# A scan kernel on one core: state work placed between the large operations, and Ln, Exp and output in three successive slots

## The chip, the core and the metric

The kernel runs on one core of a Trainium2 chip. The metric is the device time of one execution in microseconds (us). Each time below is the median of three to seven executions of the same kernel; runs that are compared were made in turn on the same chip. An execution can fall into a slower state (over 1.5% above the fastest of its kernel). Medians are over all runs, ratios over the fast ones alone.

A profile names the engines PE (matmul), PEld (PE's weight loads), DVE (the vector engine), ACT (the scalar engine), POOL and SP. "L303" is line 303 of the kernel that the profile belongs to, so the numbers differ between kernels; the tile names do not.

## The reference

A recurrence over 2048 steps for 16 batch rows of 256 channels. Everything is float32.

```python
for b in range(batch):                        # 16
    aa, bb, pp = zeros, zeros, -1e38          # vectors of 256
    for t in range(seq_len):                  # 2048
        ww = u + k[b, t];  qq = maximum(pp, ww)
        e1, e2 = exp(pp - qq), exp(ww - qq)
        output[b, t] = (e1 * aa + e2 * v[b, t]) / (e1 * bb + e2 + 1e-08)
        ww = pp - w + k[b, t];  qq = maximum(ww, k[b, t])
        e1, e2 = exp(ww - qq), exp(k[b, t] - qq)
        aa, bb, pp = e1 * aa + e2 * v[b, t], e1 * bb + e2, qq
```

## The kernel before

The steps are cut into 16 states of 126 steps (two halves of 63) and a head of 32 steps. A state has four *pairs*; a pair is two tiles of two batch rows, so 126 x 1024 numbers of k and as many of v. The kernel goes through 66 pairs in *slots*, one new pair a slot. Four slots are one state, and the time from one state to the next is called the *period*.

In slot n the new pair goes through PE (X: two matrices times k give the logs of the weights), ACT (exp of X into the tile `ez`), DVE (`ez` times v) and PE again (`tot`: sums over the steps, collected over the four pairs of a state). Ten slots later (`LAG`) the same pair is output: `den` and `num` are matmuls over `ez`, ACT takes Ln of `den` and Exp of minus that (`rd`, the reciprocal), DVE multiplies by `num`, and POOL stores.

```python
    LAG = 10
    ...
    kpool = ctx.enter_context(tc.tile_pool(name="kpool", bufs=AHEAD))
    ezpool = ctx.enter_context(tc.tile_pool(name="ezpool", bufs=7))
    rpool = ctx.enter_context(tc.tile_pool(name="rpool", bufs=5))
    ...
            for t, x, eng in ((kr, k, SP if n <= AHEAD else POOL), (vr, v, SP)):   # loads of a pair
                K(eng.dma_start(
                    out=t[0:r, :, :], in_=x[4 * p:4 * p + 4, t0:t0 + r, :].rearrange("n t d -> t n d")))
```

Between the two, the sums of a state become the state that enters it. That is *state work*, a chain of some twenty small operations: `copy_sums` (ts, ACT), `turn_sums` (a transposition on PE into a `den` tile), `split_sums` (tsum, DVE), `state_logs` (lf, ACT), offsets and `near` (DVE), `state_weights` (w and g, ACT), `tb`, `da`, `AB` (DVE), `inject_logs` and `inject_weights` (y and phi, ACT), `carries` (DVE), `turn_carries` (PE). The state is written as two rows below the 126 steps of `ez`, by four small transfers of 8 KB each, on the queue that also brings v:

```python
    def inject(c):
        row = small.tile([128, 128], BF16, tag="row", name="row")
        K(DVE.tensor_copy(row, st.pop((c, "d"))[:, 0:128]))
        for j in range(2):
            for h in range(2):
                p = 64 * h + 32 * j
                K(SP.dma_start(out=EZ[group_of(c, j)][TC + h:TC + h + 1, 0:2, :, :].rearrange(
                                   "o q i (x c) -> o (q i x) c", c=128),
                               in_=row[p:p + 32, :]))

    def den(n):                                    # reads all 128 rows of ez: the carried rows too
        rl, ri = (NH, NH) if is_head(n) else (128, TC)
        d = bank("den", [128, 2, D])
        ...
    def recip(n):                                  # Ln, then Exp of it, at once
        ...
            K(SC.activation(rd[0:r, a, :], d[0:r, a, :], ACT.Ln, scale=RS))
            K(SC.activation(rd[0:r, a, :], rd[0:r, a, :], ACT.Exp, scale=-1.0))
```

In the timelines each engine works in exactly the order in which the program is written. With s the last slot of a state (its first pair was slot s-3, so it is output from slot s-3+10 = **s+7** on), the order of a steady slot and the places of the state work are:

```python
        work += [(s + 1, "last", split_sums), (s + 2, "first" if c else "exp", state_logs),
                 (s + 2, "sums", state_offsets), (s + 2, "sums", state_weights), (s + 2, "pool", first),
                 (s + 2, "act", inject_logs), (s + 3, "exp", inject_weights),
                 (s + 3, "pool", carries), (s + 3, "last", turn_carries), (s + 3, "last", inject)]
    ...
    for n in range(NP + LAG + 1):
        ...
        exps(n);  small_work(n, "exp");  sums(n - 1);  round_k(n + 1);  small_work(n, "sums")
        num(qp, 0);  den(q);  recip(q);  mult(qp, 0);  num(qp, 1);  small_work(n, "pool")
        times_v(n);  mult(qp, 1);  store(qp);  logs(n + 1);  cast_v(n + 1)
        small_work(n, "dve");  small_work(n, "act");  small_work(n, "last")
```

(That loop is shortened: conditions for the first and last slots are left out.)

Of the kernel before, what the change touches and what calls it, by code (L numbers as in the profile page):

```python
# [7 lines left out]
F32 = mybir.dt.float32  # L8
# [14 lines left out]
def kernel(  # L23
# [363 lines left out]
    def state_offsets(c):  # L387
        lf = st.pop((c, "lf"))
        for h in range(2):
            i = 2 * c + h  # L390
            K(DVE.scalar_tensor_tensor(S[:, i + 1], S[:, i], 0.0, lf[:, h], ALU.max, ALU.add))
        near = tiny.tile([128, 3, 32], F32, tag="near", name="near")
        K(DVE.tensor_scalar(near, S[:, 2 * c:2 * c + 3], NEAR, -NEAR, ALU.min, ALU.max))
        st[c, "near"] = near
# [24 lines left out]
    def state_step(c, h):  # L419
        if h == 0:  # L420
            t = st.pop((c, "t"))[:, 0:4].rearrange("p (q h) x -> p q h x", q=2)
            tb = small.tile([128, 2, 2, 32], F32, tag="tb", name="tb")
            K(DVE.scalar_tensor_tensor(tb, by_two(st.pop((c, "w"))), 1.0, t, ALU.min, ALU.mult))  # L423
            st[c, "tb"] = tb
        cur = AB[c]
        if h == 1:
            AB[c + 1] = small.tile([128, 2, 2, 32], F32, tag="AB", name="AB")
        da = tiny.tile([128, 2, 32], F32, tag=f"da{h}", name=f"da{h}")
        K(DVE.tensor_add(da, cur[:, :, h], st[c, "tb"][:, :, h]))
        K(DVE.scalar_tensor_tensor(cur[:, :, 1] if h == 0 else AB[c + 1][:, :, 0], by_two(st[c, "g"][:, h + 1]), 1.0,  # L430
                                   da, ALU.min, ALU.mult))
# [11 lines left out]

    def carries(c):

        ab = tiny.tile([128, 4, 2, 16], BF16, tag="ab16", name="ab16")
        f, f2 = st.pop((c, "phi")), tiny.tile([128, 2, 32], F32, tag="phi2", name="phi2")
        K(DVE.scalar_tensor_tensor(f2, st[c, "g"][:, 0:2], 1.0, f, ALU.max, ALU.min))
# [43 lines left out]
    def recip(n):  # L492
        r = NH if is_head(n) else TC
        i = tiles_of(n)
        rd = rpool.tile([128, 2, D], F32, tag="rd", name="rd")
        d = DEN.pop(n)
        for a in ((0, 1), (1, 2)) if n == NP - 1 else ((0, i),):
            a = slice(*a)
            K(SC.activation(rd[0:r, a, :], d[0:r, a, :], ACT.Ln, scale=RS))  # L499
            K(SC.activation(rd[0:r, a, :], rd[0:r, a, :], ACT.Exp, scale=-1.0))  # L500
        RD[n] = rd
# [36 lines left out]

    later = {}
    for c in range(-1, NST):  # L540
        s = last_of[c]
        work = [(s + 1, "sums", copy_sums), (s + 1, "last", turn_sums)]
        first, second = lambda c: state_step(c, 0), lambda c: state_step(c, 1)
        if c < 0:
            work += [(s + 2, "sums", split_sums), (s + 2, "act", state_logs),
                     (s + 3, "exp", state_weights), (s + 3, "pool", state_start)]
        else:
            work += [(s + 1, "last", split_sums), (s + 2, "first" if c else "exp", state_logs),
                     (s + 2, "sums", state_offsets), (s + 2, "sums", state_weights), (s + 2, "pool", first),
                     (s + 2, "act", inject_logs), (s + 3, "exp", inject_weights),  # L550
                     (s + 3, "pool", carries), (s + 3, "last", turn_carries), (s + 3, "last", inject)]
            if c + 1 < NST:
                work.append((s + 4 if c else s + 3, "pool", second))
            else:

                work = [(s + 1, "act", copy_sums), (s + 2, "sums", turn_sums), (s + 2, "sums", split_sums),
                        (s + 3, "first", state_logs), (s + 3, "sums", state_offsets), (s + 3, "act", state_weights),
                        (s + 3, "last", first), (s + 4, "act", inject_logs), (s + 4, "act", inject_weights),
                        (s + 4, "last", carries), (s + 5, "pool", turn_carries), (s + 5, "pool", inject)]
        for slot, where, f in work:  # L560
            later.setdefault((slot, where), []).append((f, c))

    def small_work(n, where):
        for f, c in later.pop((n, where), []):
            f(c)

    for slot, where, f in ((0, "exp", matrices_for_sums), (1, "pool", matrices_for_head),
                           (4, "dve", matrices_for_outputs),
                           (5, "dve", more_matrices_for_outputs)):
        later.setdefault((slot, where), []).append((lambda c, f=f: f(), None))  # L570
# [9 lines left out]
    for n in range(NP + LAG + 1):  # L580
        q, qp = out_at.get(n), out_at.get(n - 1)
        live, out_q, out_qp = n < NP, q is not None, qp is not None
# [4 lines left out]
        small_work(n, "first")  # L587
        if live:
            exps(n)
        elif out_q:  # L590
            den(q)
            recip(q)
        small_work(n, "exp")
        if 0 < n <= NP:
            sums(n - 1)
# [57 lines left out]
```

## Time and profile before

| | before |
|---|---|
| median of 3 runs (range) | 331.96 us (329.77 to 335.51) |
| span of the profiled run, mean granted clock | 332.9 us, 0.983 |
| period (copies of the sums, start to start) | 17.76 to 17.77 us, once 17.99 |
| rows issued, and needed | end of slot s+3, slot s+7: about 13 us later |

The prediction below shows the views that carry its argument. First the busy share per engine and, from the same page, the chain that ended last (what released what, followed back from the end; shares of the span by engine, then by line):

```profile
PE 284.7 (86%) x1183; PEld 136.8 (41%) x1200; DVE 284.4 (85%) x571; ACT 277.8 (83%) x310; POOL 114.0 (34%) x162
...
PE 43%; DVE 27%; DMA 10%; ACT 10%; issue 6%; SPq 1%; POOL 0%; POOLq 0%; DVEq 0%; ACTq 0%
PE X L287 12%; PE num L509 11%; PE tot L349 10%; DMA vr<-in_v_dram 7%; DVE ez L319 6%; PE den L488 5%; DVE rd L517 5%; DVE km L271 5%; ACT ez L303 5%; PE den L365 4%; DVE vb L311 4%; DMA kr<-in_k_dram 3%; DVE tsum L372 2%; ACT rd L499 1%; DVE tb L423 1%
```

Three engines are within 3% of each other, and the chain wanders over all of them; the only transfers of any size in it are v loads, nearly all of it the last ones (7%), and the first k loads (3%). Of the rows only one of the last is in it, with 2.8 us. Second, the transfers by kind (destination from source, queue, how many, KB each, median us from issue to landing), and under it the view of the row tile in the steady part, 85 to 265 us (minimum, median, maximum to landing):

```profile
vr<-in_v_dram SPq DMA_DIRECT2D x60, 512.0 KB, 5.1
...
ez<-row SPq DMA_DIRECT2D x64, 8.0 KB, 6.4
```

```profile
DMA to landing us min/median/max: 5.0/6.5/7.2
```

In the steady part 8 KB take 6.5 us, where the first rows of the run, at 44 us, land after 1.9; with about 13 us of distance, 7.2 us is hidden. The 5.1 of the v loads must not be set beside it: the trace tells the landing of six v loads only, all issued in the first 26 us.

### The profile page before, as it was taken

What the parts mean: (1) busy time and instruction counts of PE and PEld (TensorE: products, weight loads), DVE (VectorE), ACT (ScalarE), POOL (GpSimd) and SP (SyncE); (2) the same over time, 40 slices, a digit from 0 to 9 for tenths busy, and PEclk for the clock granted to TensorE, in tenths of its full rate; (3) what the DMA queues carried; (4) which work ended last, traced back from release to release, by engine and by line L of the source; (5) the groups of instructions that cost most, each with busy time, mean ns of one, the idle gap of its engine ahead of it and who ended that gap; (6) DMA issues with size and microseconds to landing.
All of it is one profiled execution on the core that took longest, in us unless ns stands there. A gap on an engine that the chain in (4) does not pass through costs nothing.

```text
span 332.9 us, 4061 instructions
## 1 busy us (share of the span) xinstructions
PE 284.7 (86%) x1183; PEld 136.8 (41%) x1200; DVE 284.4 (85%) x571; ACT 277.8 (83%) x310; POOL 114.0 (34%) x162
## 2 busy tenths in 40 slices
PE   0786988799999998999999999999998999599580
PEld 0333544344445453545454444444453445234230
DVE  2888798989898989999999989898989997777560
ACT  2656699699999999998999999999999997798780
POOL 6211224514243434425243434243334433022231
PEclk9999799999999999999999999999999999999987
DMA  7999859899999999999999999999999999545855
GB/s 251 227 348 349 280 184 323 254 326 321 341 366 343 375 336 372 328 364 347 376 343 374 344 365 348 349 368 343 364 342 373 317 274 322 196 130 166 252 166 166
DMA packets 59120, 102.47 MB, mean 308 GB/s; under 512 B 7610, under 2 KB 43162, under 8 KB 59098
## 3 DMA queue, kind: packets, MB, share of 16 engines
q0 software_dynamic: 19232, 65.27, 56.2%
q1 hardware_dynamic: 39858, 36.93, 36.5%
q8 instruction: 9, 0.15, 0.2%
q14 instruction: 13, 0.11, 0.1%
q10 hardware_dynamic: 8, 0.00, 0.0%
HBM read 68.10 MB, written 33.55 MB: 305 GB/s over the span
## 4 chain that ended last, share of the span: by engine, by line
PE 43%; DVE 27%; DMA 10%; ACT 10%; issue 6%; SPq 1%; POOL 0%; POOLq 0%; DVEq 0%; ACTq 0%
PE X L287 12%; PE num L509 11%; PE tot L349 10%; DMA vr<-in_v_dram 7%; DVE ez L319 6%; PE den L488 5%; DVE rd L517 5%; DVE km L271 5%; ACT ez L303 5%; PE den L365 4%; DVE vb L311 4%; DMA kr<-in_k_dram 3%; DVE tsum L372 2%; ACT rd L499 1%; DVE tb L423 1%
## 5 line engine op out<-in xcount | busy, mean ns | idle before, releaser
L535 POOL DMA_DIRECT2D out_dram<-rd x64 | 58.6, 916 | 173.6 <-ACT rd L500 79.3
L303 ACT ACTIVATE ez<-X 128x2048 bf16<-128x2048 f32 x58 | 107.9, 1860 | 4.4 <-PE X L287 4.4
L517 DVE TENSOR_TENSOR rd<-num,rd 126x512 f32<-126x512 f32 (+1 forms) x131 | 89.1, 686 | 9.1 <-issue 3.4
L319 DVE TENSOR_TENSOR ez<-ez,vb 126x2048 bf16<-126x2048 bf16 (+1 forms) x66 | 79.9, 1211 | 2.4 <-ACT ez L301 1.8
L499 ACT ACTIVATE rd<-den 126x1024 f32<-126x1024 f32 (+2 forms) x67 | 67.0, 1000 | 9.0 <-PE den L488 8.3
L500 ACT ACTIVATE rd<-rd 126x1024 f32<-126x1024 f32 (+2 forms) x67 | 69.6, 1039 | 2.1
L287 PE MATMUL X<-km,NLE 128*128 128x512 f32 x128 | 52.6, 493 | 14.9 <-DVE km L271 13.8
L128 POOL DMA_DIRECT2D kr<-in_k_dram x61 | 47.8, 784 | 30.3 <-DVE km L271 11.6
L349 PE MATMUL tot<-ez,OHV 126*48 126x512 bf16 x128 | 50.1, 391 | 8.3 <-DVE ez L319 8.3
L509 PE MATMUL num<-ez,LfN 128*128 128x512 bf16 x128 | 49.5, 387 | 6.5 <-DVE rd L517 6.3
L349 PE MATMUL tot<-ez,OHE 128*48 128x512 bf16 x128 | 51.1, 399 | 0.0
L509 PE MATMUL num<-ez,IdN 126*128 126x512 bf16 (+1 forms) x131 | 50.3, 384 | 0.0
L271 DVE CAST km<-kr 126x1024 fp32r<-126x1024 f32 x64 | 44.8, 700 | 4.5 <-ACT km L205 4.5
L311 DVE CAST vb<-vr 126x1024 bf16<-126x1024 f32 (+1 forms) x66 | 45.4, 688 | 3.6 <-DMA vr<-in_v_dram 3.6
L287 PE MATMUL X<-km,NLZ 128*128 128x512 f32 x128 | 41.0, 403 | 0.0
L488 PE MATMUL den<-ez,Id 126*128 126x512 bf16 (+1 forms) x131 | 39.6, 382 | 0.9
L488 PE MATMUL den<-ez,Lf 128*128 128x512 bf16 x111 | 34.9, 383 | 5.3 <-DMA ez<-row 2.3
L287 PEld LDWEIGHTS X<-km,NLE 128*128 128x128 f32 x128 | 24.1, 196 | 27.4 <-DVE km L271 9.5
L287 PEld LDWEIGHTS X<-km,NLZ 128*128 128x128 f32 x128 | 24.7, 193 | 6.1 <-ACT ez L301 0.3
L349 PEld LDWEIGHTS <-OHE 128*48 128x48 bf16 x128 | 13.2, 104 | 33.6 <-issue 26.9
L509 PEld LDWEIGHTS <-LfN 128*128 128x128 bf16 x128 | 12.4, 97 | 32.1 <-issue 23.2
L509 PEld LDWEIGHTS <-IdN 126*128 126x128 bf16 (+1 forms) x131 | 12.9, 98 | 23.7 <-issue 21.9
(101 smaller groups left out, 205.0 us busy)
## 6 DMA issues: line engine op xcount, KB each, us to landing
out_dram<-rd POOLq DMA_DIRECT2D x63, 504.0 KB, 7.2
vr<-in_v_dram SPq DMA_DIRECT2D x60, 512.0 KB, 5.1
kr<-in_k_dram POOLq DMA_DIRECT2D x57, 512.0 KB, 7.9
vr<-in_v_dram SPq DMA_DIRECT2D x4, 504.0 KB
kr<-in_k_dram POOLq DMA_DIRECT2D x4, 504.0 KB, 11.3
kr<-in_k_dram SPq DMA_DIRECT2D x3, 512.0 KB, 6.5
ez<-row SPq DMA_DIRECT2D x64, 8.0 KB, 6.4
kr<-in_k_dram SPq DMA_DIRECT2D x3, 128.0 KB
```

Source lines behind the costliest of these rows:

```text
L271: K(DVE.tensor_copy(KM[n][0:r, 0:i, :], kr_of.pop(n)[0:r, 0:i, :]))
L287: K(PE.matmul(X[q][:, i, :], m[0:kr, :], km[0:kr, i, :], start=True, stop=True))
L303: K(SC.activation(ez_of(n)[:, 0:4:2], X[2][:, :, 0:i, :], ACT.Exp))
L311: K(DVE.tensor_copy(vb[0:r, 0:i, :], vr_of.pop(n)[0:r, 0:i, :]))
L319: K(DVE.tensor_mul(ez[0:r, 1:4:2], ez[0:r, 0:4:2], vb[0:r, 0:i, :].unsqueeze(1).broadcast_to([r, 2, i, D])))
L349: K(PE.matmul(TOT[c], m[0:r, :], ez_of(n)[0:r, q, i, :], start=n == first_of[c] and i == 0 and q == 0, stop=n == last_of[c] and i == tiles ...
L488: K(PE.matmul(d[:, i, :], m[0:r, :], ez_of(n)[0:r, q, i, :], start=q == 0, stop=q == 2, skip_group_check=True))
L499: K(SC.activation(rd[0:r, a, :], d[0:r, a, :], ACT.Ln, scale=RS))
L500: K(SC.activation(rd[0:r, a, :], rd[0:r, a, :], ACT.Exp, scale=-1.0))
L509: K(PE.matmul(d, m[0:r, :], ez_of(n)[0:r, q, i, :], start=q == 1, stop=q == 3, skip_group_check=True))
L517: K(DVE.tensor_mul(RD[n][0:r, i, :], NUM.pop((n, i))[0:r, :], RD[n][0:r, i, :]))
L535: K(eng.dma_start(out=out[4 * p + a:4 * p + b, t0:t0 + TC, :].rearrange("n t d -> t n d"), in_=o[0:TC, a:b, :]))
```

## The change

The intent is that no engine has two operations in a row of which the second needs the first. The small operations of the state are spread one by one between the large ones; Ln of a pair, Exp of it and its output go into three successive slots, so that ACT always has another pair's operation in between. Nothing is added or removed on any engine. The core of the diff:

```diff
-    def recip(n):
-        ...
-            K(SC.activation(rd[0:r, a, :], d[0:r, a, :], ACT.Ln, scale=RS))
-            K(SC.activation(rd[0:r, a, :], rd[0:r, a, :], ACT.Exp, scale=-1.0))
+    def log_den(n, a=0, b=None):      # Ln alone
+    def invert(n, a=0, b=None):       # Exp alone
 ...
+        "first": ((1, "a0", copy_sums), (1, "p1", turn_sums), (1, "d5", split_sums), (2, "a0", state_logs),
+                  (2, "d4", state_offset, 0), (2, "d4", state_offset, 1), (2, "d4", state_near),
+                  (2, "a1", state_weights), (3, "d0", state_sums), (3, "d0", state_add, 0),
+                  (3, "d1", state_decay, 0), (3, "a0", inject_logs), (3, "a1", inject_weights),
+                  (4, "d0", carry_weights), (4, "d0", carries), (4, "p0", turn_carries), (4, "d1", inject),
+                  (4, "d4", state_add, 1), (4, "d5", state_decay, 1)),
+        "steady": ((1, "a0", copy_sums), (1, "p1", turn_sums), (1, "d5", split_sums), (2, "a0", state_logs),
+                   (2, "d4", state_offset, 0), (2, "d5", state_offset, 1), (3, "d0", state_near),
+                   (3, "a0", state_weights), (3, "d4", state_sums), (3, "d5", state_add, 0),
+                   (4, "d0", state_decay, 0), (4, "a0", inject_logs), (4, "a0", inject_weights),
+                   (4, "d5", carry_weights), (5, "d0", carries), (5, "p0", turn_carries), (5, "d1", inject),
+                   (5, "d4", state_add, 1), (5, "d5", state_decay, 1)),
 ...
-    for n in range(NP + LAG + 1):
-        q, qp = out_at.get(n), out_at.get(n - 1)
+    for n in range(NP + LAG + 2):
+        q, qi, qp = out_at.get(n), out_at.get(n - 1), out_at.get(n - 2)
 ...         # order of a steady slot after the change
+        exps(n);  small_work(n, "d0");  round_k(n + 1);  num(qp, 0);  small_work(n, "p0")
+        small_work(n, "d1");  small_work(n, "a0");  invert(qi);  den(q);  log_den(q)
+        mult(qp, 0);  num(qp, 1);  small_work(n, "d2");  cast_v(n + 1);  small_work(n, "d3")
+        logs(n + 1);  times_v(n);  small_work(n, "p1");  sums(n);  small_work(n, "d4")
+        mult(qp, 1);  store(qp);  small_work(n, "d5");  small_work(n, "a1")
```

(The last eight lines are put together from the new loop, without its conditions; the plans for the head and the last state are cut.) In each tuple the number is the slot after s.

## The prediction

> **What bounds the kernel now.** I read the page's busy shares (PE 86%, DVE 85%, ACT 83%: no engine stands out), then the share of busy time by windows, then the timeline of ACT and of DVE over one period, then the waits, then the end of the timeline. The kernel works in slots, one per pair of batch rows; every fourth slot starts a new state, so four slots are one period. In the timeline of ACT the copy of the sums (line 358) comes back every 17.76 us (118.64, 136.40): that is the period, 4.44 us a slot. One period by windows (columns: length, then busy us of PE, PEld, DVE, ACT, POOL, then clock, DMA share, GB/s):
>
> ```profile
> 107.20:125.00 17.80, 16.83 (x74) 8.19 (x73) 16.86 (x34) 16.64 (x19) 6.86 (x8) 1.00 1.03 356
> ```
>
> DVE and ACT are each idle only about 1 us of 17.8, DMA packets are in flight all the time. So three engines and the DMA are balanced, and what can be won is the idle microsecond plus what small work costs. ACT in the expensive slot:
>
> ```profile
> 118.64 0.58 ACT L358 ACTIVATE ts<-tot 48x512 f32<-48x512 f32 x1
> 119.11 1.01 ACT L499 ACTIVATE rd<-den 126x1024 f32<-126x1024 f32 x1
> 120.16 1.06 ACT L500 ACTIVATE rd<-rd 126x1024 f32<-126x1024 f32 x1
> 121.89 0.26 ACT L384 ACTIVATE lf<-tsum 128x64 f32<-128x64 f32 x1 [0.67 <-DVE tsum L372]
> 122.05 1.86 ACT L303 ACTIVATE ez<-X 128x2048 bf16<-128x2048 f32 x1
> 123.81 0.25 ACT L403 ACTIVATE w<-near 128x64 f32<-128x64 f32 x1
> 123.95 0.27 ACT L404 ACTIVATE g<-near 128x96 f32<-128x96 f32 x1
> 124.13 1.02 ACT L499 ACTIVATE rd<-den 126x1024 f32<-126x1024 f32 x1
> ```
>
> The reader is to see that the small log of the state stands ahead of the large exponential, and waits 0.67 us for a DVE copy; and that from Ln to Ln this slot takes 5.02 us. DVE in the same slot:
>
> ```profile
> 121.50 0.36 DVE L372 COPY tsum<-den 128x192 f32<-128x192 f32 x1 [0.29 <-PE den L365]
> ...
> 124.09 0.29 DVE L423 SCALAR_TENSOR_TENSOR tb<-w,tsum 128x128 f32<-128x128 f32 x1 [0.38 <-ACT w L403]
> 124.42 0.23 DVE L429 TENSOR_TENSOR da<-AB,tb 128x64 f32<-128x64 f32 x1
> 124.75 0.22 DVE L430 SCALAR_TENSOR_TENSOR AB<-g,da 128x64 f32<-128x64 f32 x1
> ```
>
> Each small operation waits for the one before, and DVE for ACT. The waits from 89.5 to 285 us (total, times, longest) say that it is so each time:
>
> ```profile
> ACT lf L384 <- DVE tsum L372: 6.8, 10, 0.7
> DVE tb L423 <- ACT w L403: 3.8, 10, 0.4
> ACT rd L499 <- PE den L488: 3.8, 11, 0.6
> DVE tsum L372 <- PE den L365: 2.9, 10, 0.3
> ```
>
> At the end of the kernel two waits for transfers stand on the path:
>
> ```profile
> 284.36 0.69 DVE L311 CAST vb<-vr 126x1024 bf16<-126x1024 f32 x1 [3.64 <-DMA vr<-in_v_dram]
> ...
> 313.81 0.38 PE L488 MATMUL den<-ez,Lf 128*128 128x512 bf16 x1 [2.30 <-DMA ez<-row]
> ```
>
> **What the Trainium skill says.** (1) "ScalarE: Activation LUTs", What ACT_TABLE_LOAD costs: back-to-back ACTIVATEs overlap by about 93 ns. The trace agrees where they are independent (the exponential lasts 1.86 us, the next starts 1.76 us after it) and not for Ln and its own Exp: 119.11 to 120.16 is 1.05, with a length of 1.01. (2) "Perfetto Trace Analysis", Optimizing Scalar/DVE Operations: DVE's write-acknowledgement half overlaps the next instruction. The 0.69 us products have successors 0.60 us later, but dependent da and AB stand 0.33 apart with 0.23 of length. (3) "DMA: Bandwidth & Descriptors", Specifications: about 358 GB/s of HBM per core, 435 of fabric. This trace has 350 to 361 in the steady periods and up to 376 in a slice of 8.3 us, so the first is no wall, but there is little above. (4) The same page, Why a DMA increments its semaphore: a hardware-queue transfer uses the largest number up to 16 of engines that divides its rows, so the last four v loads (126 rows) would use 14. Counted from the packets, those took 5 to 8 us each where earlier ones took about 4; the 3.64 us wait above is for one of them.
>
> **The change, part by part.** No large operation is added or removed; I compared the order on each engine.
>
> ACT: the large operations become exp(n), Exp(q-1), Ln(q), all independent of their neighbours. Ln goes from 1.05 to 1.02 - 0.09 = 0.93; a slot is 1.76 + 0.97 + 0.93 = 3.66, four are 14.64. State work (ts 0.58, lf 0.26, w 0.25, g 0.27, y 0.24, phi 0.34, less 0.09 each, plus 0.12 as phi now follows y directly) is 1.52. ACT needs 16.16 us a period; today it needs 16.58 and waits 1.18.
>
> DVE: four operations at 0.60 and one at 1.14 are 3.54 a slot, 14.16 a period. The twelve small ones last 2.90 in sum; less 0.09 each when a large one stands between them, 1.83. DVE needs 15.99; today it is 14.16 + 2.67 with dependent gaps + 0.85 of waits + 0.1 elsewhere.
>
> PE: unchanged in work, but sums move to the end of their own slot, behind X. The turning of the sums still uses the only den tile. So it waits for Ln(q), which is now the last operation of ACT's slot, and a chain sets that slot: Ln 1.02, turn 1.03, tot 0.98, num 0.43, den to its end 1.06, handovers 0.08: 4.6 us, against 5.02 today. The log of the state now comes after exp, so it no longer stretches it.
>
> Period: 4.6 for that slot; the others are ACT's 3.66 + 0.34 (w, g), + 0.52 (y, phi), + 0.49 (ts) = 4.00 + 4.18 + 4.15. Sum **16.93**, say 16.95, against 17.77: 0.82 less. From 71.7 us (where the pattern has settled) to the last exponential at 293.9, less the 3.6 of waiting, there are 12.3 periods: **-10.1 us**.
>
> Start (0 to 71.7): the first outputs come at slot 10 and loads and building of matrices rule; I take 0. Wait for v: the transfers shift along with the slots, but their queue will be fuller; +1.5 by choice. Tail (294 to 325): the last state is injected in its slot s+4, one earlier than today, so the 2.3 us wait for row should go; Ln and Exp take 1.90 instead of 2.05 a pair, times 8: 1.2, of which other waits take half. The third output slot is no added work, it only lengthens the chain by a few tenths. **-3**. Sum: 332.0 - 10.1 + 1.5 - 3 = 320.4; I add 0.6 for late transfers: **321**.
>
> **Rivals.** (A) DMA becomes the bound. A period moves 4 x 1528 KiB = 6.26 MB; at 16.95 us that is 369 GB/s, just under the best slices (372 to 376). For: the DMA share is 1.03 throughout. Against: in those slices it kept up, and no steady wait for a load exists. At 356 GB/s the period would be 17.6 and the time about 328. (B) The carried rows come late. They are now issued early in slot s+5 (today, at the end of s+3) and needed by den in slot s+7: about 8 us instead of 13. Today they land 5.0 to 14 us after issue, median 6.6, behind v in the same queue. A wait of 1 us each period would bring back the whole gain: 332. (C) rd buffers: an output is held a slot longer with the same five, leaving some 11 us from store to reuse, for landings of 6.7 to 10.3; a fuller queue would stall Ln. Half a us per period: 327. (D) Waits vanish further than I think and DVE at 15.99 or ACT at 16.16 sets the period: 312, but A forbids most of that (387 GB/s).
>
> **Range and chances.** 321, with 312 (rival D in part and a better tail) to 330 (A or B in part) for 8 in 10. Faster by over 2% means below 325.3: 0.72, as the named waits really go; within 2% 0.22, from A, B, C; slower 0.06, if row waits hit every period.
>
> **What would show it.** In the after profile: copies of the sums 16.95 us apart; no ACT wait of lf for tsum, none of tb for w; Ln followed 0.93 later; the slot with the turning at 4.6 from Ln to Ln, waiting for den; GB/s near 369; the tail without the row wait. Wrong if den waits for row in the steady part, if Ln waits for a store, if vb or km wait for loads there, or if the tail grows with its added slot.

## The result, and the profile after

| | before | after |
|---|---|---|
| median (range), same chip, 4 runs each | 332.13 us (329.77 to 335.51) | 347.47 us (344.82 to 354.78) |
| ratio after / before, 95% interval | | **1.046** (1.034 to 1.058): slower |
| span of the profiled run, mean granted clock | 332.9 us, 0.983 | 343.1 us, 0.968 |
| ACT's last large exponential starts | 293.91 us | 304.04 us |
| from there to the end of the span | 39.0 us | 39.1 us |

A ratio is the mean time of one kernel's fast runs over the mean of the other's fast runs of the same rounds, so it is not quite the ratio of the medians. One of the four runs after (354.78) was slow and is not in it.

The change cost 4.6% where 3% less had been predicted. The last exponential is 10.1 us later than before and the rest takes as long as before: the whole of the loss in the profiled run lies ahead of the last exponential. Where, the chain that ended last says, from the page after:

```profile
PE 41%; DMA 18%; DVE 16%; ACT 15%; issue 5%; SPq 0%; ACTq 0%; POOL 0%; POOLq 0%; DVEq 0%
DMA ez<-row 17%; PE X L287 10%; PE num L517 10%; PE den L495 9%; PE tot L349 8%; ACT ez L303 6%; ACT rd L504 4%; DVE rd L525 4%; DVE ez L319 4%; PE den L365 3%; DVE km L271 3%; DVE vb L311 2%; DMA crow<-in_u_dram 2%; ACT ez L301 1%; ACT rd L509 1%
```

The transfer of the rows, absent before, is the largest single item. The share is of time on the chain, from issue to landing, not of time lost. The windows of one period show that most periods are like before and a few are not. Columns: length, then busy us of PE, PEld, DVE, ACT, POOL, then clock, DMA share, GB/s:

```profile
107.20:125.00 17.80, 13.46 (x46) 5.92 (x45) 11.31 (x23) 10.87 (x12) 3.52 (x5) 0.81 0.92 298
178.30:196.00 17.70, 16.97 (x75) 8.34 (x75) 16.86 (x33) 16.50 (x19) 7.06 (x9) 1.00 1.04 356
```

The second line answers to the one before the change, engine by engine: nothing was removed. In the first, PE loses 3.5 us, DVE and ACT 5.6 each, at once, which is what a hole in the pipeline looks like, and the granted clock falls to 0.81 with it. The chain in that stretch, and PE's timeline at its end (in brackets, the idle time just before the instruction and what ended it):

```profile
101.29 0.59 ACT ts L358
101.88 0.21 SPq L471
102.09 0.05 issue
102.14 12.48 DMA ez<-row
114.62 0.14 issue
114.75 1.86 PE den L495 x4
```

```profile
114.75 1.01 PE L495 MATMUL den<-ez,Lf 128*128 128x512 bf16 x2 [4.34 <-DMA ez<-row]
```

PE was ready for `den` at 114.75 - 4.34 = 110.41 us, 8.3 us after this row was issued, as the prediction had worked out ("about 8 us instead of 13"). The row needed 12.48. PE keeps its order, so X of the next pair waits behind `den`, ACT's Ln and exp behind those, and DVE behind ACT. The landing of the rows over the steady part, and of the loads in the same queue:

```profile
DMA to landing us min/median/max: 4.5/8.0/12.9
```

```profile
vr<-in_v_dram SPq DMA_DIRECT2D x60, 512.0 KB, 10.3
...
ez<-row SPq DMA_DIRECT2D x64, 8.0 KB, 7.6
```

(The 10.3 of the v loads is again a median of five loads issued in the first 26 us.) The distance fell by 5 us and the longest landing of this stretch rose from 7.2 to 12.9. With a median of 8.0 against a distance of 8.3, the rows are late only in the upper half of the landings, and clearly so in a few: `den` waited 3.50 us at 50.27, 4.34 at 114.75, 0.86 at 152.86, 0.33 at 241.34, 0.16 at 259.00 and 5.37 at 281.76. That is 14.6 us in sum. The two long waits are not of one kind. The rows behind the 5.37, issued at 267.5, when the last v loads are in the queue, land after up to 13.9 us; in the kernel before, the rows issued at 274.3, also among the last v loads, take up to 14.0 and nobody waits for them. That hole is distance alone. The 12.9 behind the 4.34 has no counterpart in the steady part of the kernel before.

The copies of the sums (one per state) put these against the time. After minus before, state by state in order:

| copy of the sums | before, us | after, us | difference |
|---|---|---|---|
| 6th | 100.88 | 101.29 | +0.4 |
| 7th | 118.64 | 125.33 | +6.7 |
| 10th | 171.93 | 178.84 | +6.9 |
| 15th | 260.99 | 267.35 | +6.4 |
| 16th | 278.75 | 292.47 | +13.7 |
| 17th | 300.24 | 308.43 | +8.2 |

Two stretched periods (24.04 and 25.12 us instead of about 17.7) make +6.3 and +7.3, more than the 4.34 and 5.37 of waiting; presumably the emptied engines have to fill again, but the difference was not isolated. The other periods are 17.5 to 18.3, from the 7th copy to the 15th 17.75 on average, no shorter than before. At the 17th, the kernel before has had its own hole, the 3.64 us wait for v that the prediction shows; after has none there.

So the intended effect did come. The waits from 89.5 to 285 us (total, times, longest):

```profile
PEld L495 <- DMA ez<-row: 14.3, 7, 5.8
PE den L495 <- DMA ez<-row: 11.1, 5, 5.4
...
ACT ez L303 <- PE X L287: 9.4, 23, 1.5
...
DVE rd L525 <- ACT lf L384: 6.2, 10, 0.6
PE den L495 <- DVE row L467: 4.5, 10, 0.5
```

The old ones, lf for tsum (6.8) and tb for w (3.8), are down to 0.6 and 0.9 in the whole run. In their place stand those of the rows and three new groups, which the section on the prediction takes up. (The fourth line's releaser is the profile's guess: the product at 166.57 also needs `num`, whose matmul at 166.09 comes just ahead of it, while lf had no part in it.)

ACT in the slot with the turning of the sums, the one for which the prediction showed before's:

```profile
161.20 0.58 ACT L358 ACTIVATE ts<-tot 48x512 f32<-48x512 f32 x1
161.68 1.05 ACT L509 ACTIVATE rd<-rd 126x1024 f32<-126x1024 f32 x1
162.62 1.01 ACT L504 ACTIVATE rd<-den 126x1024 f32<-126x1024 f32 x1
163.97 1.88 ACT L303 ACTIVATE ez<-X 128x2048 bf16<-128x2048 f32 x1 [0.33 <-PE X L287]
165.75 0.25 ACT L384 ACTIVATE lf<-tsum 128x64 f32<-128x64 f32 x1
165.89 1.05 ACT L509 ACTIVATE rd<-rd 126x1024 f32<-126x1024 f32 x1
167.38 1.02 ACT L504 ACTIVATE rd<-den 126x1024 f32<-126x1024 f32 x1 [0.44 <-PE den L495]
168.88 1.88 ACT L303 ACTIVATE ez<-X 128x2048 bf16<-128x2048 f32 x1 [0.47 <-PE X L287]
```

Here lf is in its new place behind the large exponential and costs 0.14; Ln stands 0.94 after the Exp of another pair; the step from Ln to Ln is 4.76, where before had 5.02. But ACT now waits for X on both sides of it.

### The profile page after: what moved, and what is told of

It is laid out like the page before. It is cut to its first block, busy times and chain, and to the rows that moved or that the text cites.

```text
span 343.1 us, 4065 instructions
## 1 busy us (share of the span) xinstructions
PE 286.8 (84%) x1183; PEld 137.4 (40%) x1200; DVE 283.6 (83%) x571; ACT 274.1 (80%) x310; POOL 114.2 (33%) x162
## 4 chain that ended last, share of the span: by engine, by line
PE 41%; DMA 18%; DVE 16%; ACT 15%; issue 5%; SPq 0%; ACTq 0%; POOL 0%; POOLq 0%; DVEq 0%
DMA ez<-row 17%; PE X L287 10%; PE num L517 10%; PE den L495 9%; PE tot L349 8%; ACT ez L303 6%; ACT rd L504 4%; DVE rd L525 4%; DVE ez L319 4%; PE den L365 3%; DVE km L271 3%; DVE vb L311 2%; DMA crow<-in_u_dram 2%; ACT ez L301 1%; ACT rd L509 1%
## 5 line engine op out<-in xcount | busy, mean ns | idle before, releaser
L543 POOL DMA_DIRECT2D out_dram<-rd x64 | 53.7, 839 | 177.2 <-issue 124.6
L509 ACT ACTIVATE rd<-rd 126x1024 f32<-126x1024 f32 (+2 forms) x67 | 68.9, 1028 | 0.3
L287 PE MATMUL X<-km,NLE 128*128 128x512 f32 x128 | 53.6, 501 | 14.5 <-DVE km L271 11.2
L128 POOL DMA_DIRECT2D kr<-in_k_dram x61 | 53.0, 869 | 32.7 <-DVE km L271 15.6
L495 PE MATMUL den<-ez,Lf 128*128 128x512 bf16 x112 | 35.4, 386 | 20.6 <-DMA ez<-row 14.6
L311 DVE CAST vb<-vr 126x1024 bf16<-126x1024 f32 (+1 forms) x66 | 48.8, 739 | 0.0
L271 DVE CAST km<-kr 126x1024 fp32r<-126x1024 f32 x64 | 44.0, 688 | 4.6 <-ACT km L205 4.6
L287 PE MATMUL X<-km,NLZ 128*128 128x512 f32 x128 | 41.7, 408 | 0.2 <-ACT ez L301 0.2
L495 PEld LDWEIGHTS <-Lf 128*128 128x128 bf16 x128 | 11.8, 98 | 36.5 <-DMA ez<-row 14.3
## 6 DMA issues: line engine op xcount, KB each, us to landing
vr<-in_v_dram SPq DMA_DIRECT2D x60, 512.0 KB, 10.3
```

The source lines that it names most:

```text
L271: K(DVE.tensor_copy(KM[n][0:r, 0:i, :], kr_of.pop(n)[0:r, 0:i, :]))
L287: K(PE.matmul(X[q][:, i, :], m[0:kr, :], km[0:kr, i, :], start=True, stop=True))
L311: K(DVE.tensor_copy(vb[0:r, 0:i, :], vr_of.pop(n)[0:r, 0:i, :]))
L495: K(PE.matmul(d[:, i, :], m[0:r, :], ez_of(n)[0:r, q, i, :], start=q == 0, stop=q == 2, skip_group_check=True))
L509: K(SC.activation(RD[n][0:r, a:b, :], RD[n][0:r, a:b, :], ACT.Exp, scale=-1.0))
L543: K(eng.dma_start(out=out[4 * p + a:4 * p + b, t0:t0 + TC, :].rearrange("n t d -> t n d"), in_=o[0:TC, a:b, :]))
```

## Experiments

Two theories of the loss were put up first. **R** (for rows): the carried rows are issued a slot later and not read later, and nothing else matters much. **Q** (for queue): the rows land later than before because of what stands ahead of them in their queue. A third possibility is that the new order itself is slower, by its longer output chain or by something in the slot. A difference whose interval holds 1 is not leaned on.

### Is it the rows? Taking their wait away in both orders

**e3_rows not waited for.** The four transfers are made as before, but into a spare tile, and `num` reads 126 rows of `ez` and of its matrix. `den` still reads 128 rows, but no transfer writes into them any more. Nothing can wait for a row. The result is wrong (the carried state is missing).

```diff
     def inject(c):
-                K(SP.dma_start(out=EZ[group_of(c, j)][TC + h:TC + h + 1, 0:2, :, :].rearrange(
+                if (j, h) == (0, 0):
+                    spare = tiny.tile([128, 2, 4, D], BF16, tag="spare", name="spare")
+                K(SP.dma_start(out=spare[124 + 2 * j + h:125 + 2 * j + h, 0:2, :, :].rearrange(
 ...     # in num alone
-        rl, ri = (NH, NH) if is_head(n) else (128, TC)
+        rl, ri = (NH, NH) if is_head(n) else (TC, TC)
```

> Wrong result on purpose: the changed kernel sends its carried rows, in the same slots and with the same transfers, into a spare tile that nobody reads, so den can't wait for them (num reads 126 rows of ez in place of 128). Theory R: 332 to 336 us, period about 17.5 us in the steady part, as PE is full there. If PE is not the bound, the period falls to the 16.95 us that I had predicted and the time to 322 to 327 us. Rival O: above 343 us.

Measured: 329.81 us, ratio to before 0.991 (0.985 to 0.998). Against the 347.47 of after that is 17.7 us less, or, by the two ratios, (1.046 - 0.991) x 332 = 18 us. In the steady part no period is longer than 18.1, and most are 17.5. The rows still take 5.9/8.6/12.6 us to land, so the late landing is there and costs nothing once no one waits. The whole of the loss comes with waiting for rows.

**e11_control.** The same two edits in the kernel before (wrong too): without row waits, which order is faster?

> Wrong result on purpose, control for the same edit of the changed kernel: the kernel before sends its carried rows into a spare tile that nobody reads. There only the wait of 2.3 us in the tail can go: 329 to 333 us, period 17.77 as before. If more goes, the rows cost the kernel before something too, and the gain of the new order (17.52 against 17.77 us a period) has to be counted anew.

Measured: 330.09 us, 0.991 (0.983 to 0.999), period 17.77. Without row waits the two orders are equal. The 6th copy of the sums starts at 98.87 in e3 and at 101.13 in e11, the 16th at 275.28 and 278.81: 2.3 us gained at the start and 1.3 over ten periods, which are 17.64 on average against 17.77. (After that both wait for v loads, 3.45 us in e3, 0.90 and 1.98 in e11.) The tail from the last large exponential to the end takes 39.6 and 37.0. So the new order does gain 0.13 us a period, and gives it back, with the gain of the start, in a tail that is 2.6 us longer and in that wait.

### Is it the distance? Moving the issue, or the reader, by one slot

**e1_the old order with the rows a slot later.** In the kernel before, carries, turn and injection move from s+3 to s+4. Theory R says that before must then lose as after did.

```diff
-                     (s + 3, "pool", carries), (s + 3, "last", turn_carries), (s + 3, "last", inject)]
+                     (s + 4, "pool", carries), (s + 4, "last", turn_carries), (s + 4, "last", inject)]
```

> The kernel before, but the carried rows are multiplied, turned and sent one slot later (s+4 in place of s+3), which is about the distance to den (some 8 us) that the changed kernel has. Theory R (the 10 us of the profiled loss are waits of den for late rows): den waits for rows appear in the steady part, in two or more periods for 3 us or more, and the time rises from 332 to 338 to 346 us. Rival O (the new order of large operations itself costs the time, the rows only show it): no waits of note, 330 to 334 us.

Measured: 345.43 us, 1.036 (1.028 to 1.044). The total is what R said, the way there only half. The first rows are waited for (3.7 us at 51.9) and so are some at the end (1.6 at 297.6, 2.9 at 324), but in the steady part the rows land after 4.2/5.7/7.1 us and none is waited for. About 4 us of the loss is that the period rose from 17.77 to 18.11, with the small operations in another slot. This run taught that these small operations could not be moved for free, and that a row issued later does not by that land later. Landings of over 10 us in the steady part stand only in runs of the new order (after, e3, e4, e8, e12, e13), and not in all of them: e2 and e6 have at most 8.8 and 8.2, the runs of the old order at most 8.7.

**e2_the new order with the rows a slot earlier.** All states but the last use the plan of the first one, which injects in s+4.

```diff
-        for slot, where, f, *args in PLANS["head" if c < 0 else "first" if c == 0 else
+        for slot, where, f, *args in PLANS["head" if c < 0 else "first" if c + 1 < NST else
                                            "last" if c + 1 == NST else "steady"]:
```

> The changed kernel with the state plan of the first chunk used for every chunk but the last: rows are sent in slot s+4 in place of s+5, the rest of the order is unchanged. Theory R: the waits of den for rows of 4.3 and 5.4 us are gone; 347 falls to 333 to 337 us. Rival O: it stays above 343 us.

Measured: 343.54 us, 1.025 (1.015 to 1.034). The steady row waits are gone, but the period is 18.43, because that plan puts w straight behind near (ACT waits for it 1.2 us a period, 1.6 at most); the first rows are still waited for, 4.1 us at 50. The expectation was missed: earlier rows were bought with a denser chain.

**e6_another earlier plan.** tb, add and decay together in s+3, y and phi at its end, rows in s+4:

```diff
-                   (3, "a0", state_weights), (3, "d4", state_sums), (3, "d5", state_add, 0),
-                   (4, "d0", state_decay, 0), (4, "a0", inject_logs), (4, "a0", inject_weights),
-                   (4, "d5", carry_weights), (5, "d0", carries), (5, "p0", turn_carries), (5, "d1", inject),
+                   (3, "a0", state_weights), (3, "d4", state_sums), (3, "d4", state_add, 0),
+                   (3, "d4", state_decay, 0), (3, "a1", inject_logs), (3, "a1", inject_weights),
+                   (4, "d0", carry_weights), (4, "d0", carries), (4, "p0", turn_carries), (4, "d1", inject),
```

> The changed kernel with another steady plan that sends the rows in slot s+4 in place of s+5, by putting the first state step behind times_v of slot s+3 and the two small activations behind Ln of the same slot. Unlike the earlier run with the first chunk's plan, ACT does not wait for the state there. Theory R: no den wait for rows in the steady part, period 17.5 to 17.8 us, 330 to 335 us in all, level with the kernel before. If the placing of the state work costs as much as it did in the plan of the first chunk (period 18.43), 340 us or more.

Measured: 348.28 us, 1.041 (1.034 to 1.049), period 18.70. No row is waited for in the steady part, and it is as slow as after. The view of waits names the new one:

```profile
ACT y L438 <- DVE AB L433: 8.8, 10, 0.9
```

y is at the end of ACT's slot and needs the last of three dependent DVE operations, so ACT idles 0.9 each period. Both ways of getting the rows out earlier make two engines wait for each other; the steady plan of the change had avoided that by paying with the row's distance.

**e13_the reader a slot later.** The third way to the distance leaves the state work alone and outputs each pair a slot later. The `ez` tiles then live longer: one more of them, paid for with one k buffer, with single buffers for ts and tsum, and with a spare matrix reused.

```diff
-    LAG = 10
+    LAG = 11
-    kpool = ctx.enter_context(tc.tile_pool(name="kpool", bufs=AHEAD))
+    kpool = ctx.enter_context(tc.tile_pool(name="kpool", bufs=AHEAD - 1))
-    ezpool = ctx.enter_context(tc.tile_pool(name="ezpool", bufs=7))
+    ezpool = ctx.enter_context(tc.tile_pool(name="ezpool", bufs=8))
-        Lx = matrix("Lx", F32)
+        Lx = IO
-        ts = small.tile([48, D], F32, tag="ts", name="ts")
+        ts = tiny.tile([48, D], F32, tag="ts", name="ts")
-        t = small.tile([128, 6, 32], F32, tag="tsum", name="tsum")
+        t = tiny.tile([128, 6, 32], F32, tag="tsum", name="tsum")
-    out_at = {n + (LAG - 4 if is_head(n) else LAG): n for n in range(NP)}
+    out_at = {n + (LAG - 5 if is_head(n) else LAG): n for n in range(NP)}
```

> The changed kernel in its own order, but the outputs of a pair come 11 slots after its exponential in place of 10, with an eighth ez buffer for it (paid by three kr buffers in place of four and single ts and tsum buffers). The rows then have some 12 us in place of 8. Theory R: no den wait for rows in the steady part or at the start, period 17.5 to 17.6 us; one more slot in the tail costs some 2 us; 347 falls to 331 to 335 us. If it stays above 340 us, the distance is not the cause.

Measured, with a correct result: **330.91 us** (329.58 to 330.99), ratio to before 0.991 (0.987 to 0.995). It is the fastest correct version: 0.9% (0.5 to 1.3) under the kernel before, and by the two ratios (1.046 - 0.991) x 332 = 18 us under the change. Its rows land as late as those of the change, as the view of the row tile shows:

```profile
DMA to landing us min/median/max: 7.3/8.7/12.4
```

But only one of them is waited for, 0.21 us at 269. One period by windows:

```profile
178.30:195.85 17.55, 16.87 (x75) 8.23 (x73) 16.71 (x33) 16.37 (x19) 6.99 (x9) 1.00 1.04 359
```

The busy times are those of the change's undisturbed period. The same landings, one slot more of distance, and the loss is gone, at the same 0.991 as e3, where nothing waits at all. This is the run that shows R for the whole kernel with a correct result; e3 takes away the wait alone.

### Why do the rows land later? Their queue

**e5_v loads on ACT's queue.** Both the 512 KB v loads and the rows are issued by SP. In this run the v loads from slot 9 on are issued by ACT.

```diff
-            for t, x, eng in ((kr, k, SP if n <= AHEAD else POOL), (vr, v, SP)):
+            for t, x, eng in ((kr, k, SP if n <= AHEAD else POOL), (vr, v, SP if n <= 8 else SC)):
```

> The changed kernel; the v loads from the ninth on are issued from ACT's queue, so the carried rows are alone on SP's. Plan and order are unchanged. Theory Q (the rows come late because they stand behind v loads in one queue): the rows land some 3 to 5 us after issue in place of 8.0 in the steady part, den does not wait for them there, 347 falls to 330 to 336 us (ACT's sequencer may lose up to 0.3 us a slot to the issues). Rival S (all engines of the DMA are full, whichever queue the rows are in): they land after 7 us or more and the time stays above 342 us.

Measured: 337.88 us, 1.008 (1.000 to 1.015), with one steady row wait of 0.29 us (at 167.91) and periods of 17.5 to 18.1. The row tile in the steady part:

```profile
DMA to landing us min/median/max: 5.1/6.7/8.4
```

The long landings are cut from 12.9 to 8.4 us, the median only from 8.0 to 6.7. The Trainium skill, "DMA: Bandwidth & Descriptors", Queues, rings and completion order, states that each of the 16 engines takes the descriptors of one queue in order and goes round between the queues; SP and ACT have a queue each. The trace agrees with that: in the change v is issued 3.0 us ahead of the rows in the same queue (4.2 in the kernel before), and in the event at 102.14, 8 of the 128 packets of the rows started at 113 us when the other 120 had started by about 110; 8 is what one engine of 16 carries if they are shared evenly. So Q is true of the upper tail, and a row with a queue of its own still needs 6.7 us while the engines are full (DMA share 1.03); in the change, the rows sent at 292.7, after the last v load, land after 1.9 to 3.4 us. What is left against before is the first rows (4.73 us at 52.1) and the v loads, which are now late at the end (1.49 and 2.46 us).

How far the usual row lands later is less sure than the views look. They miss one of the four rows of a state, the first before the change and the last after it. Counted from the packets (128 of 256 B a state), the last packet ends 7.6 us after the first issue before the change (7.0 to 7.8) and 8.0 after it (6.6 to 12.1): the median hardly moved, the upper tail did. That the v loads themselves land later in the new order is not shown.

**e7_both:** e6 and e5 together.

> Rows sent in slot s+4 by the other plan and v loads on ACT's queue. If either alone takes away the waits, this gains no more than 2 us over the better of the two; if each takes away half, it is the best of the four, 328 to 332 us.

Measured: 348.94 us, 1.045 (1.036 to 1.053), period 18.70. As in e6, ACT's wait for AB sets the period, and a better queue cannot help where no row is waited for.

**e9_queue, first rows and last loads.** e5, with the first state's chain pulled together so that its rows go out in s+3, and with the last v loads (126 rows) split into 112 and 14.

```diff
-            for t, x, eng in ((kr, k, SP if n <= AHEAD else POOL), (vr, v, SP)):
-                K(eng.dma_start(
+            for t, x, eng in ((kr, k, SP if n <= AHEAD else POOL), (vr, v, SP if n <= 8 else SC)):
+                for a, b in ((0, 112), (112, r)) if r < 128 and x is v else ((0, r),):
+                    K(eng.dma_start(
 ...     # in the plan "first"
-                  (2, "d4", state_offset, 0), (2, "d4", state_offset, 1), (2, "d4", state_near),
+                  (2, "d2", state_offset, 0), (2, "d2", state_offset, 1), (2, "d2", state_near),
 ...
-                  (3, "d1", state_decay, 0), (3, "a0", inject_logs), (3, "a1", inject_weights),
-                  (4, "d0", carry_weights), (4, "d0", carries), (4, "p0", turn_carries), (4, "d1", inject),
+                  (3, "d0", state_decay, 0), (3, "a0", inject_logs), (3, "a0", inject_weights),
+                  (3, "d3", carry_weights), (3, "d3", carries), (3, "p1", turn_carries), (3, "d4", inject),
```

> Candidate to beat both: the changed kernel with v loads on ACT's queue, the rows of the first chunk sent about half a slot sooner (its state work closer together in slots where no engine is full), and each of the last four v loads split into 112 and 14 rows. Against the run with ACT's queue alone: the 4.7 us wait of den for the first rows falls to 2 us or less, the 1.5 and 2.5 us waits for the last v loads go; 338 falls to 329 to 333 us, 1% under the kernel before at best.

Measured: 336.80 us (333.66 to 340.25), 1.013 (1.003 to 1.022). Missed: no better than e5. The landings of rows that the trace tells in the steady part are of one state only (7.2/7.5/7.8 us); one row is waited for (1.62 us at 73.9). The first rows are no longer waited for, so that edit worked; at the end ACT's large exponentials at 267.32 and 274.30 wait 1.20 and 2.92 us for v transfers, which ACT's own queue now issues in two pieces each. With three edits at once the run does not show what each is worth.

### Is it the order? What the new slot is worth

**e8_outputs in two slots.** e6 with Exp straight behind Ln again and the output a slot later, as before. If the third output slot is worth something, this must be slower.

```diff
-        q, qi, qp = out_at.get(n), out_at.get(n - 1), out_at.get(n - 2)
+        q, qi, qp = out_at.get(n), None, out_at.get(n - 1)
 ...
                 log_den(q)
+                invert(q)
```

> On the plan with rows in s+4: Exp follows its own Ln in the same slot again and the outputs come one slot later, as in the kernel before, so the three-slot outputs are undone alone. If the third slot is worth what I predicted (Ln 0.10 us shorter a slot, ACT on the path), this is 3 to 6 us slower than the run with rows in s+4; if ACT is not the bound, within 2 us.

Measured: 341.41 us, 1.021 (1.013 to 1.029), period 18.39: *faster* than e6 by 6.9 us, against the expectation. ACT's wait of y for AB falls from 0.9 to 0.3 us a period, and the first rows are no longer waited for (3.9 us in e6). Separating Ln and Exp is thus not a gain of its own; in this plan it is a loss, and what it is worth in the change's own plan no run tells.

**e4_less for PE.** e3 with one of the four `tot` matmuls of a slot left out (wrong). If PE set e3's period of 17.5, it would fall by 4 x 0.22 = 0.88.

```diff
+                if not head and (i, q) == (0, 1):
+                    continue
```

> Wrong result on purpose: as the run before, and one of the four matmuls for the sums left out in each slot (some 0.22 us of PE a slot, 0.88 us a period). Theory P (PE bounds the steady part of the changed kernel): the period falls from about 17.5 to 16.7 to 16.9 us, the time by 8 to 11 us against the run before. Rival D (the DMA bounds it, at about 355 GB/s): less than 2 us.

Measured: 327.83 us, 0.985 (0.977 to 0.992), period 17.30: 0.2 less, not 0.88. PE is not alone at the limit.

**e12_less for PE and DVE.** e4, and the second product of `rd` at half width (wrong).

```diff
-        K(DVE.tensor_mul(RD[n][0:r, i, :], NUM.pop((n, i))[0:r, :], RD[n][0:r, i, :]))
+        x = D if is_head(n) or i == 0 else D // 2
+        K(DVE.tensor_mul(RD[n][0:r, i, 0:x], NUM.pop((n, i))[0:r, 0:x], RD[n][0:r, i, 0:x]))
```

> Wrong result on purpose: as the run without the wait for rows and with one matmul for the sums less a slot (period 17.30 us), and the second product of each slot made half as wide (some 0.27 us of DVE a slot, 1.07 a period). If PE and DVE bound the period together, hand over hand, it falls to 16.4 to 16.7 us and the time by 7 to 11 us. If the DMA bounds it (17.30 us are 362 GB/s), it falls by 0.1 at most.

Measured: 324.93 us, 0.975 (0.967 to 0.983), period 17.11, another 0.2 where 1.07 of DVE's time was freed. Waits for v loads turn up in the steady part, at 366 GB/s over a period, and ACT is busy for 16.1 us of 17.1. So freeing PE and DVE by about a microsecond each did not bring the period to the predicted 16.95; whether ACT or the transfers hold it at 17.1 was not isolated.

### The last waits of the kernel before

Two of before's waits, for the last v loads (3.6 us) and for the last row (2.3 us), were counted on in the prediction. What are they worth?

**e10_last v loads split** in the kernel before: 112 + 14 rows instead of 126.

```diff
-                K(eng.dma_start(
-                    out=t[0:r, :, :], in_=x[4 * p:4 * p + 4, t0:t0 + r, :].rearrange("n t d -> t n d")))
+                for a, b in ((0, 112), (112, r)) if r < 128 and x is v else ((0, r),):
+                    K(eng.dma_start(
+                        out=t[a:b, :, :], in_=x[4 * p:4 * p + 4, t0 + a:t0 + b, :].rearrange("n t d -> t n d")))
```

> The kernel before, with the last four v loads (126 rows) each split into 112 and 14 rows. If the number of engines of the DMA that such a load uses[...] made them slow, the 3.6 us wait of vb near the end goes and the time falls by 2 to 4 us; if they were slow because the queue was full, nothing changes.

Measured: 332.62 us, 0.997 (0.990 to 1.005). The v wait is gone, as the page on DMA cited in the prediction would have it (126 rows on 14 engines; no view here shows the number of engines itself). But the next wait has grown from 2.30 to

```profile
313.49 0.61 PE L489 MATMUL den<-ez,Lf 128*128 128x512 bf16 x1 [4.40 <-DMA ez<-row]
```

and `den` runs at nearly the same moment as before (313.81).

**e14_and the last rows sooner**, in the kernel before:

```diff
-                        (s + 3, "last", first), (s + 4, "act", inject_logs), (s + 4, "act", inject_weights),
-                        (s + 4, "last", carries), (s + 5, "pool", turn_carries), (s + 5, "pool", inject)]
+                        (s + 3, "last", first), (s + 3, "last", inject_logs), (s + 3, "last", inject_weights),
+                        (s + 4, "exp", carries), (s + 4, "sums", turn_carries), (s + 4, "sums", inject)]
```

> The kernel before with the last chunk's rows sent most of a slot sooner and the last v loads split. The wait of 2.3 to 4.4 us of den for the last rows in the tail goes; 328 to 331 us, some 1% under the kernel before, which is at the edge of what three rounds can tell.

Measured: 331.98 us, 0.997 (0.992 to 1.002). Both waits are gone from the profile and the time is the same within the interval; other waits of 1.7 to 2.8 us stand in the tail now. Inconclusive: 5.9 us of waits by the profile were worth less than 1%.

### Together

| run | ratio to before | steady period, us | row waits in the steady part |
|---|---|---|---|
| after | 1.046 | 17.5 to 18.3, two of 24 to 25 | 4.3, 5.4 and small ones |
| e1 old order, rows s+4 | 1.036 | 18.11 | none |
| e2, e6 new order, rows s+4 | 1.025, 1.041 | 18.43, 18.70 | none |
| e5 v on ACT's queue | 1.008 | 17.5 to 18.1 | one of 0.3 |
| e3 new order, rows not waited for | 0.991 | 17.5 to 18.1 | (none possible) |
| e11 old order, rows not waited for | 0.991 | 17.77 | (none possible) |
| e13 new order, read a slot later | 0.991 | 17.54 to 17.83 | one of 0.2 |

## Why the prediction was wrong, point by point

**The step that failed is the weight of rival B.** The prediction saw the cause: rows "issued early in slot s+5" and needed "about 8 us instead of 13" later, behind v in the same queue, with landings of "5.0 to 14 us after issue, median 6.6". It then took "a wait of 1 us each period" as its size, made it cost the gain alone ("332"), and gave slower 0.06. Its own numbers said more: with a distance of 8, part of a spread of 5 to 14 is late, by up to 6 us each, and one late row is enough to hold `den`. What came is not a microsecond each period but two holes of 6 to 7 us, 3.5 us at the first rows, and a few small waits: 14.6 us of waiting for `den`, 17.7 us of time (e3). The median was the wrong statistic; a wait comes from the tail. And the landing was taken as given, where the tail of it moved too, from 7.2 to 12.9 in the steady part; but for the larger of the two holes the 14 us of the kernel before, which the prediction had read, were enough.

**Period: "Sum 16.93" was 17.5 to 17.8.** This too failed, by about 0.7 us a period. Without waits for rows the average of ten periods is 17.64 (e3) or 17.58 (e13) against 17.77: a gain of 0.13 to 0.19 us a period instead of 0.82, so about 2 of the 10.1 us. So even without rival B the change would have won 0.9% (e3) and not 3%. Three terms were mis-sized.

- *PE.* The sum of slots has ACT's work in the three ordinary slots (4.00, 4.18, 4.15) and a chain of PE in the fourth (4.6). Measured from Ln to Ln: 4.76 for the slot with the turning, then 4.53, 4.21 and 4.14, so 17.64. The slot after the turning is the one that lost 0.5: PE is behind and X is late (the 0.47 in the timeline of ACT above). PE's own ordinary slot is

```profile
170.37 0.59 PE L495 MATMUL den<-ez,Lf 128*128 128x512 bf16 x2
...
174.26 0.59 PE L495 MATMUL den<-ez,Lf 128*128 128x512 bf16 x2
```

  3.89 us from `den` to `den`; in the slot with the turning 5.44 (num to num, 160.43 to 165.87). Three slots of 3.89 and one of 5.44 are 17.1, of which 0.45 is PE's wait for DVE's copy of the row out of the only `den` tile. That alone is more than 16.93. The prediction left PE at "unchanged in work" and never added up its slots.
- *DVE.* "DVE needs 15.99" counts each small operation 0.09 less wherever a large one was to stand between two. But the operations of the end of one slot (d5) and of the start of the next (d0) adjoin again: da at 173.70 and AB at 174.01 are 0.31 apart with 0.21 of length. The small ones take 2.40 us a period and not 1.83. And some casts of v grew:

```profile
157.52 0.98 DVE L311 CAST vb<-vr 126x1024 bf16<-126x1024 f32 x1
...
167.18 0.68 DVE L311 CAST vb<-vr 126x1024 bf16<-126x1024 f32 x1
...
171.16 0.68 DVE L311 CAST vb<-vr 126x1024 bf16<-126x1024 f32 x1
```

```profile
158.00 0.80 POOL L128 DMA_DIRECT2D kr<-in_k_dram  x1
...
171.13 1.01 POOL L128 DMA_DIRECT2D kr<-in_k_dram  x1
```

  The long one lies beside POOL issuing a load; the one at 167.18 does not; the one at 171.16 does and stays short, but there POOL's issue takes 1.01 instead of 0.80. So it is throughout: of the 39 casts from 85 to 265 us 13 took over 0.8 us, all beside POOL with the load's issue at 0.77 to 0.84; 16 short ones stood beside POOL too, with an operation of POOL's of 1.0 us or more. In the kernel before, none of 40 casts stood beside an issue and none was long (mean over the kernel 688 ns, after 739). The Trainium skill, "SBUF — State Buffer", Who interferes with whom, states that a cast can hold a port pair that GpSimd needs, and that either one blocks while the other has it; the trace fits that, one of the two being long each time, but no run isolated it.
- *The common wall.* e4 and e12 show the rest: freeing 0.88 us of PE, then 1.07 of DVE, shortens the period by 0.2 each time. Rival A (356 GB/s, period "17.6 and the time about 328") described the steady part well: 356 GB/s and 17.5 to 17.8.

**Tail: "-3" was 0** (39.0 and 39.1 us). The last row is no longer waited for, as predicted. In exchange the first slot without a new pair is long (Ln at 307.29 and 310.33, 3.04 apart; before had 2.14 from 296.09 to 298.23), and the third slot, called "a few tenths", is a whole stage: e3 against e11 shows 2.6 us more tail with no row in play. Ln and Exp are not spread there either: with no large exponential between, Exp(q) follows Ln(q) as before, 2.01 a pair where before has 2.00, and not the 1.90 counted on.

**Wait for v: "+1.5" was -3.6.** In the profiled run after there is no wait for v at the end. In e3, without the holes in the pipeline, the wait is back (3.45 us), so the holes probably gave the loads time to come early; that is argued and not shown.

**What was right.** lf no longer waits for tsum nor tb for w; Ln of another pair follows Exp 0.94 later (predicted 0.93 for Ln); the slot with the turning is 4.76 (predicted 4.6, before 5.02); Ln waits for no store. And of the signs listed as making it wrong, the first one is the one that came: "if den waits for row in the steady part".

What stays open: why single rows of the new order land so late in the steady part (at 101.6, eight packets of 128 start 4 us after the others), what holds the period of e12 at 17.1, and what each edit of e9 is worth.

## What to carry to other kernels

When a change moves a producer, work out the distance to its reader for every transfer on the way, and set it against the longest landing in the trace, not the median: 8.3 us of distance against landings of 4.5/8.0/12.9, and of 13.9 near the end, cost 4.6%; with one slot more nothing was lost. Where a small transfer must arrive in time, try moving the reader too (deeper buffers), and not only the chain ahead of it: here the chain was dense and the reader was free to move. A queue of its own only trimmed the tail. When several engines are within a few per cent of each other, add up each one's slot with its gaps before promising what a removed wait is worth.

## What the Trainium skill lacked or had wrong

- "DMA: Bandwidth & Descriptors" gives latencies of single transfers; it has nothing on how long a small transfer needs among full queues. Here, in the steady part, 8 KB took a median of 6.5 us and at most 7.2 in the old order, 8.0 and 12.9 in the new one, and 6.7 and 8.4 with a queue that it did not share with the large loads.
- The same page, Rules for kernel authors, says that spreading transfers over the issuing engines doesn't help bandwidth. For bandwidth nothing here speaks against it, but for latency it did help: moving the v loads off the rows' queue took the ratio from 1.046 to 1.008. The rule counts only issue time as saved.
- The same page's rule on how many engines a transfer uses is not contradicted: splitting 126 rows into 112 and 14 removed the 3.6 us wait for v. It brought no time (0.997), since the next wait took its place.
- "Perfetto Trace Analysis" has the overlap of the write acknowledgement for DVE; the section does not say that it holds only between independent operations (that can only be inferred from the place of the semaphore in the page's timeline of an instruction). Here dependent small ones stand 0.31 us apart with 0.21 of length, and the small operations took 2.40 us a period in place of 1.83.
- "SBUF — State Buffer" agrees on casts beside GpSimd (where they overlap, either the cast takes 0.8 to 1.0 us in place of 0.68, or POOL's operation 1.0 or more), as far as a trace without an experiment can say.
